# A 128-byte pad among the constants, and one weight load issued ahead of one adaLN load

## The chip, the cores and the metric

The kernel runs on one core of one Trainium2 chip. The metric is the time of one execution on the device in microseconds (us). A second number, the span, is what the profiler saw from the first instruction to the last; what lies around it is the start and end of the program.

## What is computed

A decoder trunk of two layers on 256 tokens of width 2048, all in float32. Cut to what matters here:

```
for layer in range(2):
    shift, scale, gate = split(silu(c) @ ada_w[layer] + ada_b[layer], 3)
    h = x * (1 + scale) + shift
    if layer == 0:
        y = ssd_mixer(h, ...)       # h @ in_w (2048 x 10304), conv, scan, gate, @ out_w
    else:
        y = dilated_mixer(h, ...)   # h @ in_w, attention, gate, @ out_w
    x = layer_norm(ALPHA * x + (1 + gate) * y)
    if layer == 0:
        k, v = split(x @ kv_w, 2)
```

`c` is one vector, so `silu(c) @ ada_w` is a product of a vector with 2 x 3 x 16 tiles of 128 output columns. Everything else of weight is a product of 256 rows with a large matrix.

## The kernel before

**Products.** A product is made from three float32r products: each weight is split into a rounded high half and a remainder, each activation as well, and high x high, high x low and low x high are summed in PSUM. A weight comes as pieces of 128 x 1024 (512 KB), each covering two k-tiles of 128 rows and 512 columns, or four k-tiles and 256 columns. `load_piece` (L86 to L90) puts a piece into one of six buffers `raw`; `split` (L97 to L102) has ScalarE copy it into one of four buffers `whi` (L99) and VectorE subtract that into one of four `wlo` (L101). SyncE's queue issues these loads. `cm_piece` (L150 to L152) and `cm_wide` (L181, L184) hold the weights as the stationary operand and stream the activations `actT`; `tm_mults` (L212 to L214) holds the activations and streams the weights. `SHORT` moves `whi` and `wlo` by 16 elements within their buffers where weights are stationary; `LONG` does not.

**adaLN.** `ada_load` (L287) brings one tile of 128 output columns, 128 x 2048 (1 MB), into `araw`; `ada_dot` (L294) multiplies it on VectorE with `cb_`, silu(c) spread over the partitions, and sums it along the row. `fetch()` issues the next of 32 such loads: scale and shift for k-tile 0, scale and shift for k-tile 1, and so on. `h_step()` takes the next of them in the same order: its dot, and after a shift the two ScalarE steps L499 (h = x * scale + shift) and L501 (its high half into `actT`), then the low half on VectorE (L503).

**The beginning (to about 160 us).** While h is still being made k-tile by k-tile, products are already begun on what is there. A table `order` lists 58 pieces: b4, b6, h, z2, z1, b2, x1, h and so on, where b, x and z are column blocks of in_w and h the two blocks that run along with every k-tile. The first three pieces are loaded in halves (L534, L537). A piece's product that ends before the last k-tile is put away from PSUM by ScalarE (L634, reported there for all of these evictions, first time) or added on VectorE (L632). DMAs are issued in the order of the code, each waiting for the landing of the one eight places before it and for its buffer to be free: loads of `raw` have six buffers, loads of `araw` two buffers in each of two pools. The code just before the loop over `order` writes out the first loads and steps by hand.

**Later stages.** From about 162 us the rest of the first layer (scan, gate, out_w), the shared keys and values, and the second layer follow. Their pieces are loaded and split ahead in the same buffers; gate loads of layer 0 and all adaLN loads of layer 1 run in the background.

**Memory.** Pools lie one behind the other in a partition: first `cons` (`cb_`, `adab`, `prm`, `cc`, `magic`, `mod0`, `mod1`), then `wp` with `raw`, `whi`, `wlo`, then `act` with `actT`, and the rest. In the built kernel the first `raw` begins at byte 28800 of the partition, `whi` at 53376, `wlo` at 70784, `actT` at 88192: each 128 past a multiple of 256. The buffers of `whi` and of `wlo` follow each other at 4352 bytes, 17 x 256. `u0` and `u1` are taken from the other end of the memory.

Of the kernel before, what the change touches and what calls it, by code (L numbers as in the profile page):

```python
# [9 lines left out]
F32 = mybir.dt.float32  # L10
# [8 lines left out]
P = 128  # L19
# [30 lines left out]
def trunk(ctx, tc, xT, x, c, par, cst, bias, lnrow, ada, wdt, win, wxs, wout, wk, wv, wbin, wbout, out):  # L50
# [3 lines left out]
    cons = ctx.enter_context(tc.tile_pool(name="cons", bufs=1))  # L54
# [23 lines left out]
    ident = cc[:, CI:CI + 128]  # L78
    tri = cc[:, CT:CT + 128]
    ones = cc[:, CM:CM + 128]  # L80
    SHORT, LONG = (16, 16), (0, 0)

    def rows(t, b):
# [3 lines left out]
    def load_piece(src):  # L87
        raw = wp.tile([P, 1024], F32, name="raw", bufs=6)
        nc.sync.dma_start(raw, src)
        return raw  # L90
# [194 lines left out]
    def ada_load(pool, layer, kind, ct):  # L285
        raw = pool.tile([P, D], F32, name="araw", bufs=2)
        nc.sync.dma_start(raw, ada[layer, KIND.index(kind), ct])  # L287
        return raw
# [44 lines left out]
    with ExitStack() as cA:  # L333
# [15 lines left out]
        with ExitStack() as cS:  # L349
# [78 lines left out]
            with ExitStack() as c0:  # L428
# [31 lines left out]
                def fetch():  # L460
                    i = len(raws)
                    if i < len(cols):
                        raws.append(ada_load((wp1, pe)[i // 2 % 2], *cols[i]))

                def fetch_x(kt):
                    xts[kt // 2] = pe.tile([P, 2, L], F32, name="xt")
                    (nc.sync if kt else nc.scalar).dma_start(xts[kt // 2], xT[:, kt:kt + 2, :])
# [59 lines left out]
                def fetch_piece():  # L527
                    if len(pieces) < len(order):
                        k, q, _ = order[len(pieces)]
                        pieces.append(load_piece(source[k][q]))  # L530
# [46 lines left out]
                fetch()  # L577
                h_step()
                fetch_piece()
                fetch()  # L580
                fetch_x(2)
                fetch_piece()
                plain.t = h_step.t
                last = plain(1, plain(0, last))
                h_low = late.pop()
# [791 lines left out]
```

## Time and profile before

| | us |
|---|---|
| median of 3 runs | 1236.28 |
| lowest and highest | 1235.71, 1237.11 |
| the profiled execution | 1236.29 |
| its span | 1234.5 |
| TensorE matmul busy in it | 1220.3 |
| VectorE busy | 1028.0 |
| ScalarE busy | 701.6 |

The profile is of one execution. Its engines are PE (matmuls of TensorE), PEld (its weight loads), DVE (VectorE), ACT (ScalarE), POOL (GpSimd) and SP (SyncE, which issues DMAs). In the rows of a timeline the first two numbers are the start and the duration in us, L101 is line 101 of the kernel, x2 two instructions merged, and square brackets tell how long the engine had been idle and what ended that. In a table of windows each row has the stretch, its length, the busy time of each engine with the number of instructions, the granted TensorE clock (PEclk), the busy share of the 16 DMA engines, and what they moved in GB/s.

### The profile page before, as it was taken

The page shows a single profiled execution, that of the slowest core. Times are in us where ns is not written, and L with a number is a line of the kernel's source. Part 1 is how long each engine was busy: PE and PEld are TensorE (multiplying, and loading weights), DVE is VectorE, ACT ScalarE, POOL GpSimd, SP SyncE. Part 2 cuts the span into 40 slices and gives each one's busy share as a digit, 9 for nine tenths or more (in the row PEclk, how much of TensorE's full clock was granted, in tenths as well). Part 3 has the DMA queues.
Part 4 walks back from the last instruction along what each step waited for, and adds up shares of the span by engine and source line. Part 5 has one row for each costly group of instructions (what it writes and reads, how often), then busy time and mean ns, then how long its engine had stood idle before and what let it go on. Part 6 is the DMA issues. An engine that isn't in the chain of part 4 may idle for free.

```text
span 1234.5 us, 18854 instructions
## 1 busy us (share of the span) xinstructions
PE 1220.3 (99%) x7132; PEld 1049.4 (85%) x7132; DVE 1028.0 (83%) x1464; ACT 701.6 (57%) x1048; POOL 3.9 (0%) x8
## 2 busy tenths in 40 slices
PE   8999999999999999999999999999999999999998
PEld 7889988898888888888888788888888888888886
DVE  6899996999988989899778678888978876758776
ACT  3554577878597789754335545344445644445551
POOL 0000000000000000000000000000000000000001
PEclk9999999999999999999999999999999999999999
DMA  9999986687666456599998569989998774464673
GB/s 373 414 414 415 413 283 244 216 305 247 222 204 205 171 172 205 203 337 353 365 316 294 195 204 362 356 341 371 378 382 313 224 261 147 122 201 124 207 256 69
DMA packets 81372, 335.92 MB, mean 272 GB/s; under 512 B 9201, under 2 KB 9985, under 8 KB 68481
## 3 DMA queue, kind: packets, MB, share of 16 engines
q1 hardware_dynamic: 80352, 333.33, 75.0%
q0 software_dynamic: 576, 1.05, 0.6%
q8 instruction: 56, 0.92, 0.3%
q10 hardware_dynamic: 352, 0.34, 0.1%
q14 instruction: 36, 0.29, 0.1%
HBM read 331.45 MB, written 3.23 MB: 271 GB/s over the span
## 4 chain that ended last, share of the span: by engine, by line
PE 84%; DMA 6%; DVE 6%; ACT 2%; issue 1%; ACTq 0%; DVEq 0%
PE acc L181 24%; PE acc L184 12%; PE acc L213 12%; PE acc L214 12%; PE acc L212 12%; DMA raw<-in_win 5%; DVE araw L294 3%; DVE wlo L101 2%; PE py L775 1%; PE acc L150 1%; PE acc L152 1%; PE acc L151 1%; DMA araw<-in_ada 1%; ACT whi L99 1%; PE acc L985 1%
## 5 line engine op out<-in xcount | busy, mean ns | idle before, releaser
L99 ACT ACTIVATE whi<-raw 128x1024 fp32r<-128x1024 f32 x389 | 408.9, 1058 | 362.5 <-PE acc L214 130.7
L101 DVE TENSOR_TENSOR wlo<-raw,whi 128x1024 fp32r<-128x1024 f32 x389 | 469.2, 1221 | 146.8 <-ACT whi L99 139.9
L181 PE MATMUL acc<-actT,whi 128*128 128x512 f32 x1280 | 402.8, 394 | 0.0
L184 PEld LDWEIGHTS acc<-actT,wlo 128*128 128x128 f32 x1280 | 239.5, 188 | 53.5 <-DVE wlo L101 0.5
L213 PE MATMUL acc<-wlo,actT 128*128 128x512 f32 x656 | 257.3, 392 | 1.9 <-DVE wlo L101 1.9
L212 PE MATMUL acc<-whi,actT 128*128 128x512 f32 x656 | 254.0, 394 | 0.0
L184 PE MATMUL acc<-actT,wlo 128*128 128x256 f32 x1280 | 253.8, 280 | 0.0
L294 DVE SCALAR_TENSOR_TENSOR araw<-araw,cb__72 128x2048 f32<-128x2048 f32 x95 | 217.0, 2284 | 5.2 <-DMA araw<-in_ada 4.7
L181 PEld LDWEIGHTS acc<-actT,whi 128*128 128x128 f32 x1280 | 193.9, 188 | 0.4
L214 PE MATMUL acc<-whi,actT 128*128 128x512 f32 x432 | 168.8, 391 | 0.0
L213 PEld LDWEIGHTS acc<-wlo,actT 128*128 128x128 f32 x656 | 123.2, 188 | 28.7 <-DVE wlo L101 3.6
L212 PEld LDWEIGHTS acc<-whi,actT 128*128 128x128 f32 x656 | 122.6, 188 | 25.1 <-ACT s L634 0.8
L150 PE MATMUL acc<-actT,whi 128*128 128x256 f32 x372 | 103.7, 283 | 2.9 <-ACT s L634 2.0
L152 PE MATMUL acc<-actT,wlo 128*128 128x256 f32 x372 | 102.4, 283 | 1.7 <-DVE wlo L101 1.6
L151 PE MATMUL acc<-actT,whi 128*128 128x256 f32 x372 | 103.6, 281 | 0.0
L214 PEld LDWEIGHTS acc<-whi,actT 128*128 128x128 f32 x432 | 81.1, 188 | 16.6
L214 PE MATMUL acc<-whi,ylo 128*128 128x512 f32 x224 | 87.6, 391 | 0.0
L150 PEld LDWEIGHTS acc<-actT,whi 128*128 128x128 f32 x372 | 70.3, 190 | 4.2 <-ACT s L634 2.4
L152 PEld LDWEIGHTS acc<-actT,wlo 128*128 128x128 f32 x372 | 69.5, 190 | 2.7 <-DVE wlo L101 2.7
L151 PEld LDWEIGHTS acc<-actT,whi 128*128 128x128 f32 x372 | 71.3, 192 | 0.2
L214 PEld LDWEIGHTS acc<-whi,ylo 128*128 128x128 f32 x224 | 42.1, 188 | 8.7
L733 ACT ACTIVATE seg<-cbc,cumT 128x128 f32<-128x128 f32 x128 | 41.1, 390 | 2.6 <-PE py L775 2.1
(311 smaller groups left out, 1151.1 us busy)
## 6 DMA issues: line engine op xcount, KB each, us to landing
araw<-in_ada SPq DMA_DIRECT2D x96, 1024.0 KB, 7.4
raw<-in_win SPq DMA_DIRECT2D x109, 512.0 KB, 5.7
raw<-in_wout SPq DMA_DIRECT2D x64, 512.0 KB, 5.8
raw<-in_wbin SPq DMA_DIRECT2D x64, 512.0 KB, 4.0
raw<-in_wxs SPq DMA_DIRECT2D x48, 512.0 KB, 4.4
raw<-in_wv SPq DMA_DIRECT2D x48, 512.0 KB, 6.8
raw<-in_wk SPq DMA_DIRECT2D x48, 512.0 KB, 7.2
cbc<-cumd SPq DMA_DIRECT2D x16, 512.0 KB, 4.9
```

The costliest lines, as they stand in the source:

```text
L99: copied.append(S.activation(hi, raw, AF.Copy))
L101: latest.append(V.tensor_tensor(lo, raw, hi.bitcast(F32), op=ALU.subtract))
L150: T.matmul(o, hi[:, k, c_], ahi[:, kt, :], start=first, stop=False, skip_group_check=True)
L151: T.matmul(o, hi[:, k, c_], alo[:, kt, :], start=False, stop=False, skip_group_check=True)
L152: T.matmul(o, lo[:, k, c_], ahi[:, kt, :], start=False, stop=kt == k1 - 1, skip_group_check=True)
L181: T.matmul(ps[n], hi[:, k, n * P:n * P + P], both(kt), start=kt == 0, stop=False, skip_group_check=True)
L184: T.matmul(ps[n][:, 0, :], lo[:, k, n * P:n * P + P], high(kt), start=False, stop=kt == KT - 1, skip_group_check=True)
L212: T.matmul(o, h_, hi[:, k, :], start=kt == k0, stop=False, skip_group_check=part)
L213: T.matmul(o, h_, lo[:, k, :], start=False, stop=False, skip_group_check=part)
L214: end = T.matmul(o, l_, hi[:, k, :], start=False, stop=kt == k1 - 1, skip_group_check=part)
L294: return V.scalar_tensor_tensor(raw, raw, 1.0, cb_, op0=ALU.mult, op1=ALU.mult, accum_out=mod[layer][:, ct, j:j + 1])
L733: S.activation(seg[:, hh, b, :], cbc[:, hh, b, :], AF.Relu, bias=cumT[:, b, h0 + hh:h0 + hh + 1], scale=-1.0)
```

## The change

Two edits.

```
     ones = cc[:, CM:CM + 128]
+    cons.tile([P, 32], F32, name="pad")
     SHORT, LONG = (16, 16), (0, 0)
...
                 fetch()
                 h_step()
                 fetch_piece()
+                fetch_piece()
                 fetch()
                 fetch_x(2)
-                fetch_piece()
                 plain.t = h_step.t
```

The first adds a tile of 128 bytes per partition, which nothing reads or writes, behind `cc`. Everything allocated behind it moves up by 128 bytes: `raw` begins at 28928, `whi` at 53504, `wlo` at 70912, `actT` at 88320, all multiples of 256. `cb_`, `adab`, `prm`, `cc`, `u0` and `u1` stay where they were. Tiles that stood at other distances move too: with `SHORT`, the stationary weights begin 64 bytes past a multiple of 256 and no longer 192.

The second moves the load of the sixth piece of `order` (b2, k-tiles 0 and 1) ahead of one `fetch()` and of `fetch_x(2)`. By the count of the calls, that `fetch()` is the sixth adaLN load, the shift tile of the third k-tile; the scale tile of the same k-tile has been issued by the `fetch()` between the two `h_step()` calls, and stays ahead.

SyncE's queue, from the fourth piece on. `raw_198` is the fourth piece, `raw_211` the fifth, `raw_217` the sixth, `raw_255` the seventh; `araw_203` is the fifth adaLN load, `araw_213` the sixth, `araw_257` the seventh; `xt_215` is x for k-tiles 2 and 3. Before:

```order
L89 DMA raw_198<-in_win 128x1024
L287 DMA araw_203<-in_ada 128x2048
L89 DMA raw_211<-in_win 128x1024
L287 DMA araw_213<-in_ada 128x2048
L467 DMA xt_215<-in_xT 128x512
L89 DMA raw_217<-in_win 128x1024
L89 DMA raw_255<-in_win 128x1024
L287 DMA araw_257<-in_ada 128x2048
```

After, where the added line makes every line number one larger and the buffers are numbered anew (`raw_214` is the sixth piece, `araw_216` the sixth adaLN load):

```order
L90 DMA raw_199<-in_win 128x1024
L288 DMA araw_204<-in_ada 128x2048
L90 DMA raw_212<-in_win 128x1024
L90 DMA raw_214<-in_win 128x1024
L288 DMA araw_216<-in_ada 128x2048
L468 DMA xt_218<-in_xT 128x512
L90 DMA raw_256<-in_win 128x1024
L288 DMA araw_258<-in_ada 128x2048
```

One load has passed two others; from the seventh piece on the queue is as before.

ScalarE at the same place. `whi_345` is the high half of the sixth piece, `s2` and `sz` are what z2 and z1 are put away into (`acc_322`, `acc_323` and `acc_351`, `acc_352` in PSUM), `htmp_340` is h of k-tile 2. Before:

```order
L99 ACTIVATE whi_318<-raw_211 128x1024
L99 ACTIVATE whi_345<-raw_217 128x1024
L499 ACTIVATE htmp_340<-xt_215,mod0_79 128x256
L634 ACTIVATE s2_95<-acc_322 128x512
L501 ACTIVATE actT_83<-htmp_340 128x256
L634 ACTIVATE s2_95<-acc_323 128x512
L99 ACTIVATE whi_367<-raw_255 128x1024
L634 ACTIVATE sz_113<-acc_351 128x512
L634 ACTIVATE sz_113<-acc_352 128x512
L99 ACTIVATE whi_405<-raw_259 128x1024
```

After:

```order
L100 ACTIVATE whi_319<-raw_212 128x1024
L100 ACTIVATE whi_346<-raw_214 128x1024
L635 ACTIVATE s2_96<-acc_323 128x512
L635 ACTIVATE s2_96<-acc_324 128x512
L100 ACTIVATE whi_368<-raw_256 128x1024
L500 ACTIVATE htmp_341<-xt_218,mod0_80 128x256
L635 ACTIVATE sz_114<-acc_352 128x512
L502 ACTIVATE actT_84<-htmp_341 128x256
L635 ACTIVATE sz_114<-acc_353 128x512
L100 ACTIVATE whi_406<-raw_260 128x1024
```

Putting z2 away now stands right behind the sixth piece's high half, and h of k-tile 2 behind the seventh's.

VectorE there. `wlo_346` is the low half of the sixth piece, `araw_213` the sixth adaLN dot, `mod0` takes its sum. Before:

```order
L101 TENSOR_TENSOR wlo_319<-raw_211,whi_318 128x1024
L294 SCALAR_TENSOR_TENSOR araw_213,mod0_79<-araw_213,cb__72 128x2048
L299 TENSOR_TENSOR mod0_79<-mod0_79,adab_73 128x2
L101 TENSOR_TENSOR wlo_346<-raw_217,whi_345 128x1024
L503 TENSOR_TENSOR actT_83<-htmp_340,actT_83 128x256
L101 TENSOR_TENSOR wlo_368<-raw_255,whi_367 128x1024
L294 SCALAR_TENSOR_TENSOR araw_257,mod0_79<-araw_257,cb__72 128x2048
```

After:

```order
L102 TENSOR_TENSOR wlo_320<-raw_212,whi_319 128x1024
L102 TENSOR_TENSOR wlo_347<-raw_214,whi_346 128x1024
L295 SCALAR_TENSOR_TENSOR araw_216,mod0_80<-araw_216,cb__72 128x2048
L300 TENSOR_TENSOR mod0_80<-mod0_80,adab_73 128x2
L102 TENSOR_TENSOR wlo_369<-raw_256,whi_368 128x1024
L504 TENSOR_TENSOR actT_84<-htmp_341,actT_84 128x256
L295 SCALAR_TENSOR_TENSOR araw_258,mod0_80<-araw_258,cb__72 128x2048
```

The sixth piece's low half has passed the sixth dot and its bias, and the dot of the seventh adaLN load keeps its place behind the seventh piece. On TensorE the products stand in the order of before; only the first two of the sixth piece's accumulators alternate a little differently (24 matmuls of 256 columns either way).

More of the change, by code (lines that the diff above doesn't have):

```diff
@@ L80, in trunk @@
     ones = cc[:, CM:CM + 128]
+    cons.tile([P, 32], F32, name="pad")
     SHORT, LONG = (16, 16), (0, 0)
@@ L579, in trunk @@
                 fetch_piece()
+                fetch_piece()
                 fetch()
                 fetch_x(2)
-                fetch_piece()
                 plain.t = h_step.t
```

## The prediction

> **What bounds the kernel.** The page first: span, engines, the DMA slices, the chain of what ended last.
>
> ```profile
> span 1234.5 us, 18854 instructions
> PE 1220.3 (99%) x7132; PEld 1049.4 (85%) x7132; DVE 1028.0 (83%) x1464; ACT 701.6 (57%) x1048; POOL 3.9 (0%) x8
> ...
> DMA  9999986687666456599998569989998774464673
> ...
> PE 84%; DMA 6%; DVE 6%; ACT 2%; issue 1%; ACTq 0%; DVEq 0%
> ```
>
> The chain is 84% matmuls, so over most of the program TensorE's pace is the time. The DMA row is full in the first five slices (31 us each), so the beginning has another limit. Windows over the beginning and the stage behind it:
>
> ```profile
> 40.00:127.00 87.00, 85.30 (x538) 76.07 (x538) 81.09 (x87) 46.10 (x60) 0.00 (x0) 1.00 1.02 414
> 127.00:162.00 35.00, 33.88 (x273) 32.63 (x272) 33.09 (x37) 17.32 (x22) 0.00 (x0) 1.00 0.99 395
> 162.00:560.00 398.00, 396.88 (x2644) 339.84 (x2643) 360.33 (x615) 308.02 (x520) 0.00 (x0) 1.00 0.68 231
> ```
>
> From 40 to 127 us the DMA engines are never idle (share 1.02, 414 GB/s) and DVE is 93% busy; from 162 on DMA has room and PE does not. The end of the beginning, in the chain by time and in DVE's timeline:
>
> ```profile
> 113.77 13.26 DMA araw<-in_ada
> 127.03 0.02 issue
> 127.05 2.31 DVE araw L294 x2
> ...
> 160.36 1.24 DVE wlo L101
> ```
>
> ```profile
> 46.38 1.22 DVE L101 TENSOR_TENSOR wlo<-raw,whi 128x1024 fp32r<-128x1024 f32 x1
> 47.73 2.29 DVE L294 SCALAR_TENSOR_TENSOR araw<-araw,cb__72 128x2048 f32<-128x2048 f32 x1
> ...
> 124.44 2.50 DVE L101 TENSOR_TENSOR wlo<-raw,whi 128x1024 fp32r<-128x1024 f32 x2
> 127.05 2.29 DVE L294 SCALAR_TENSOR_TENSOR araw<-araw,cb__72 128x2048 f32<-128x2048 f32 x1
> ```
>
> An adaLN load lands at 127.03 and its dot starts at 127.05, 0.11 us after DVE was free (124.44 + 2.50 = 126.94). Behind that, DVE works nearly without a gap to 161.60, and TensorE's unbroken chain starts on that last remainder. The same meeting stands at 47.73, 0.13 us after DVE was free (46.38 + 1.22 = 47.60). So what ends the beginning is the 126 us that a full DMA system needs for everything queued up to that adaLN load, plus 34.6 us of DVE (127.05 to 161.60). The rest, 1073 us, is PE.
>
> **The moved load.** No instruction is added or removed; one issue on SP passes two others. What waits on it, in the timelines of SP and ACT, and of PE (last row):
>
> ```profile
> 16.87 0.33 SPq L287 DMA_DIRECT2D araw<-in_ada  x1
> 17.48 0.33 SPq L467 DMA_DIRECT2D xt<-in_xT  x1
> 18.15 2.19 SPq L89 DMA_DIRECT2D raw<-in_win  x2
> ```
>
> ```profile
> 24.76 1.06 ACT L99 ACTIVATE whi<-raw 128x1024 fp32r<-128x1024 f32 x1 [0.65 <-DMA raw<-in_win]
> 30.17 1.06 ACT L99 ACTIVATE whi<-raw 128x1024 fp32r<-128x1024 f32 x1 [4.35 <-DMA raw<-in_win]
> 31.14 0.58 ACT L499 ACTIVATE htmp<-xt,mod 128x256 f32<-128x256 f32 x1
> 31.63 0.57 ACT L634 ACTIVATE s<-acc 128x512 f32<-128x512 f32 x1
> ```
>
> ```profile
> 32.25 0.38 PE L150 MATMUL acc<-actT,whi 128*128 128x256 f32 x1 [1.95 <-ACT s L634]
> ```
>
> ACT sits 4.35 us before the sixth piece's high half, with z2's eviction (L634, 31.63) queued behind it; PE idles 1.95 us for that eviction. The piece lands behind the sixth adaLN load (1.05 MB) and xt (0.26 MB). At 414 GB/s these are 2.5 and 0.6 us, so it lands about 3.2 us earlier, near 27.0, and its high half ends at 28.1; z2 is put away by 29.3. PE had no work left at 30.30 (32.25 - 1.95), and now has it: 1.95 us back. It gets more, since the stall is followed by a slow clock:
>
> ```profile
> 32.00:34.00 2.00, 1.75 (x9) 1.75 (x10) 0.94 (x3) 2.00 (x5) 0.00 (x0) 0.68 1.04 426
> 34.00:36.00 2.00, 2.00 (x12) 2.00 (x11) 2.00 (x2) 1.78 (x3) 0.00 (x0) 0.50 0.99 404
> 36.00:38.00 2.00, 2.00 (x18) 2.00 (x18) 2.00 (x3) 0.19 (x1) 0.00 (x0) 0.96 1.04 413
> ```
>
> Lost clock: 2 x (0.32 + 0.50 + 0.04) = 1.7 us. PE is then up to 3.7 us earlier at 38 us. The other side: the sixth adaLN load lands 0.52 MB later, 1.3 us, and its dot moves from 28.16 to about 29.4.
>
> ```profile
> 28.16 2.29 DVE L294 SCALAR_TENSOR_TENSOR araw<-araw,cb__72 128x2048 f32<-128x2048 f32 x1 [1.08 <-DMA araw<-in_ada]
> ...
> 33.97 1.23 DVE L101 TENSOR_TENSOR wlo<-raw,whi 128x1024 fp32r<-128x1024 f32 x1 [1.00 <-ACT whi L99]
> 35.11 2.28 DVE L294 SCALAR_TENSOR_TENSOR araw<-araw,cb__72 128x2048 f32<-128x2048 f32 x1
> ```
>
> On DVE the remainder of the sixth piece (1.23) runs before that dot, in a gap. Then dot (to 31.7), bias, and the seventh piece's remainder: its high half follows its landing at 31.4 and ends near 32.5, so the remainder runs to 33.7 and the next dot starts near 34.4 instead of 35.11: 0.7 us ahead. PE's earliness may also spare DVE a wait near 50 us. None of it reaches the end: at 47.73 DVE has only 0.13 us before it meets the landing, at 127.05 only 0.11, and the DMA system moves the same bytes in the same order from the seventh piece on, at a share that was 1.02 already. A lead of 0.7 or of 2 us is waited away at the second meeting. Term: 0 to -0.11 us. The cover is the full DMA queue; were it gone, the lead itself, some 1 to 2 us, would be the gain.
>
> **The pad.** It adds no instruction. It moves every large tile by 128 bytes, and their distances from each other not at all. No tile here stood at a multiple of 256, so the trace has no price; I bound each user by what address it could feel.
>
> DVE and ACT: the dots read `araw` against `cb_`, which stays, so here a distance changes. `araw` stood at two such distances already (128 past a multiple of 256, and 192 in the second pool of the beginning):
>
> ```profile
> L294 DVE SCALAR_TENSOR_TENSOR araw<-araw,cb__72 x95: 2272/2284/2294, 10.7 to 939.9; 128x2048 f32<-128x2048 f32 x95
> ```
>
> All 95 lie within 22 ns. I take nothing; 95 x 0.022 = 2 us either way is the bound, most of it beside PE.
>
> PE: of the cycle of four matmuls that `cm_wide` repeats, and of `tm_mults` in out_w:
>
> ```profile
> 302.00 0.62 PE L181 MATMUL acc<-actT,whi 128*128 128x512 f32 x2
> ...
> 303.39 0.62 PE L181 MATMUL acc<-actT,whi 128*128 128x512 f32 x2
> ...
> 306.16 0.62 PE L181 MATMUL acc<-actT,whi 128*128 128x512 f32 x2
> ```
>
> ```profile
> 599.95 0.39 PE L212 MATMUL acc<-whi,actT 128*128 128x512 f32 x1
> ...
> 600.63 0.39 PE L212 MATMUL acc<-whi,actT 128*128 128x512 f32 x1
> ```
>
> One cycle of the wide product is (306.16 - 302.00) / 6 = 693 ns, one of out_w 680 ns, and both stream 1536 columns. So 13 ns of pace can hang on something, and where the operands begin is a candidate. But the wide product keeps 693 over six cycles, which at four cycles a piece cross into another buffer, 17 x 256 bytes on: the buffer's address from 256 up has no say. The pad changes a bit just below that, for both operands alike. I take nothing, and keep both ends: all 640 wide cycles at 680, or all tm cycles at 693.
>
> DMA: a row of 4 KB now starts at a multiple of 256. The Trainium skill, "DMA: Bandwidth & Descriptors", section "How a descriptor splits into AXI transactions", says a transfer must start at a multiple of 256 and that bytes before a misaligned start still cost beats: an estimate from that page is 132 beats for such a row instead of 128, 3%. If that holds for writes, the page would have the 126 us shrink by 3.8; no row here shows an aligned large load. Against it stands the Trainium skill, "SBUF — State Buffer", whose note on cachelines has 16-byte lines, so that every start here is as good as another. From the rows alone: faster DMA gains only what DVE waits for it, since DVE is busy 81.09 of 87 us. I take nothing.
>
> **Sum.** 0 - 0.1 (moved load) + 0 (pad) on the profiled 1236.29 us, which is the median of the runs (1236.28): **1236.2 us**. Its own range, 1235.2 to 1237.2, is about how far runs of one kernel lie apart.
>
> **Rivals.**
> - *The wide products lose their uneven pace.* For: 693 against 680 for equal columns. Against: the pace ignores the buffer. 640 cycles (1280 of L181, two each) x 13 ns = 8.5 us, all on PE's chain: 1227.7.
> - *DMA rows get quicker.* The landing at 127.03 comes earlier until DVE itself is the limit. DVE's waits for the early loads are 1.08 and 1.00 in the rows above and two meetings of 0.1: about 2.3 us, so 1233.9. Against: DVE at 93% has little to give. It straddles the bound of 0.2%.
> - *Slower: the tm products take the uneven pace.* Place: L212 to L214 behind 162 us, 580 cycles of three by the groups of that stretch (the whole program has 656). Price: 13 ns each, 7.5 us, so 1243.8. It decides from a third of them on (190 x 13 ns = 2.5 us). For: one pace per kind of product shows that the layout can matter. Against: as above.
>
> ```profile
> L213 PE MATMUL acc<-wlo,actT 128*128 128x512 f32 x580 | 227.4, 392 | 0.8 <-DVE wlo L101 0.8
> ```
>
> - *The change isn't what its words say.* Its load passes the third k-tile's second adaLN load, not the first. Passing the first too would hand the piece another 2.5 us and take as much from a dot, behind the same full queue: 1236.2 again.
>
> **Chances.** Forecast 0.59; words and deed differ, same time, 0.04; wide pace 0.11; DMA rows 0.10, half of it past 0.2%; tm pace 0.16. A difference of 0.2%, 2.5 us, is about what a measurement tells from none. So faster 0.11 + 0.05 = 0.16, same 0.59 + 0.04 + 0.05 = 0.68, slower 0.16. The range takes in the DMA case, half of the tm case (to about 1240.5), and leaves out the wide case and the other half: 0.19. It runs from 1231.5, which is the DMA case with another 2 us for the bound on the dots, to 1240.5.
>
> **What would show it.** Right: L99 of the sixth piece near 27 us; no PE wait of 1.95 and no clock of 0.5 near 34; DVE's adaLN dots again starting on a landing at 127; the last remainder before PE's chain near 160.4; 693 and 680 ns per cycle as before. Wrong: a DMA rate over 420 GB/s from 40 to 127 us, or another pace at 302 or 600 us.

## The result and the profile after

The changed kernel takes **1234.53 us** (median of 21 runs, 1233.1 to 1237.16) against 1236.32 for the kernel before (21 runs beside it). The ratio is 0.9986, 95% interval 0.998 to 0.9992: 1.8 us faster, a real difference, and smaller than the 0.2% that the prediction set as its bound. The forecast was 1236.2, the rival with quicker DMA rows 1233.9; the time lies nearer to the rival, and the profile shows that it is the rival that happened.

The page of the profiled execution (1234.27 us) first, span, engines and the DMA slices:

```profile
span 1232.5 us, 18855 instructions
PE 1218.7 (99%) x7132; PEld 1048.2 (85%) x7132; DVE 1027.9 (83%) x1464; ACT 701.7 (57%) x1048; POOL 3.9 (0%) x8
...
DMA  9999977687666456699988569989998774464663
```

The sixth DMA digit has gone from 8 to 7 and the seventh from 6 to 7. A digit is a slice of 31 us, too coarse for what is sought here. The windows of the beginning, with the same columns as before:

```profile
32.00:34.00 2.00, 2.00 (x20) 2.00 (x18) 1.95 (x3) 1.67 (x4) 0.00 (x0) 1.00 1.01 424
34.00:36.00 2.00, 2.00 (x19) 2.00 (x18) 2.00 (x3) 1.06 (x1) 0.00 (x0) 1.00 1.00 416
...
40.00:127.00 87.00, 83.97 (x524) 74.70 (x524) 81.08 (x85) 46.55 (x61) 0.00 (x0) 1.00 1.02 422
127.00:162.00 35.00, 34.32 (x278) 33.23 (x278) 32.63 (x39) 17.88 (x23) 0.00 (x0) 1.00 0.95 379
```

From 40 to 127 us the DMA engines are as full as before (1.02) but move 422 GB/s in place of 414. From 127 us on they have room (0.95), where they had none (0.99). The clock of 0.68 and 0.50 between 32 and 36 us is gone. VectorE's timeline at the two meetings of the prediction, and the last remainder of the beginning:

```profile
46.58 2.29 DVE L295 SCALAR_TENSOR_TENSOR araw<-araw,cb__72 128x2048 f32<-128x2048 f32 x1 [0.45 <-DMA araw<-in_ada]
...
122.92 2.36 DVE L102 TENSOR_TENSOR wlo<-raw,whi 128x1024 fp32r<-128x1024 f32 x2
125.19 2.29 DVE L295 SCALAR_TENSOR_TENSOR araw<-araw,cb__72 128x2048 f32<-128x2048 f32 x1
...
158.51 1.22 DVE L102 TENSOR_TENSOR wlo<-raw,whi 128x1024 fp32r<-128x1024 f32 x1
```

The first meeting still is one: VectorE waits 0.45 us for the landing, which comes 1.15 us earlier than before (46.58 against 47.73). The second is none any more: at 125.19 the dot follows the remainder ahead of it at once. So behind the first meeting no dot of VectorE starts on a landing, up to the last remainder. What VectorE still waits for is mostly ScalarE's high halves: 5.9 us in 11 waits from 46 to 159 us, and 5.9 us in 11 in the kernel before. The last remainder starts at 158.51 in place of 160.36: **1.85 us, the whole of the 1.8 us** between the medians. The dots of the two traces, one against the other, show where it was won: 1.15 us by the first meeting, 0.34 near 107 us, at a meeting that the prediction doesn't have, and the last 0.37 at 127.

```profile
107.46 2.29 DVE L294 SCALAR_TENSOR_TENSOR araw<-araw,cb__72 128x2048 f32<-128x2048 f32 x1
```

```profile
105.97 2.28 DVE L295 SCALAR_TENSOR_TENSOR araw<-araw,cb__72 128x2048 f32<-128x2048 f32 x1
```

Behind the last remainder TensorE's rows are those of before: a wide cycle takes (306.24 - 302.08) / 6 = 693 ns, a cycle of out_w (600.81 - 598.77) / 3 = 680 ns.

```profile
302.08 0.62 PE L182 MATMUL acc<-actT,whi 128*128 128x512 f32 x2
...
306.24 0.62 PE L182 MATMUL acc<-actT,whi 128*128 128x512 f32 x2
```

```profile
598.77 0.39 PE L213 MATMUL acc<-whi,actT 128*128 128x512 f32 x1
...
600.81 0.39 PE L213 MATMUL acc<-whi,actT 128*128 128x512 f32 x1
```

The moved load did its part where it stands. ScalarE's timeline and TensorE's waits from 26 to 52 us:

```profile
26.20 1.06 ACT L100 ACTIVATE whi<-raw 128x1024 fp32r<-128x1024 f32 x1 [0.23 <-DMA raw<-in_win]
27.16 1.26 ACT L635 ACTIVATE s<-acc 128x512 f32<-128x512 f32 x2
```

```profile
37.04 0.39 PE L153 MATMUL acc<-actT,wlo 128*128 128x256 f32 x1 [0.41 <-DVE wlo L102]
40.71 0.39 PE L153 MATMUL acc<-actT,wlo 128*128 128x256 f32 x1 [0.65 <-DVE wlo L102]
```

The sixth piece's high half starts at 26.20 in place of 30.17, and z2 is put away behind it. TensorE's wait of 1.95 us is gone; in its place stand two of 0.41 and 0.65 for VectorE.

Two edits were made at once, so the comparison alone doesn't say whether the order of the transfers or their addresses made the rows quicker.

### The profile page after: what moved, and what is told of

Its sections match the earlier page's. It is cut to its first block, busy times and chain, and to the rows that moved or that the text cites. A ratio compares the mean times of both kernels' runs of the same rounds, so it can differ in the third digit from the quotient of the medians.

```text
span 1232.5 us, 18855 instructions
## 1 busy us (share of the span) xinstructions
PE 1218.7 (99%) x7132; PEld 1048.2 (85%) x7132; DVE 1027.9 (83%) x1464; ACT 701.7 (57%) x1048; POOL 3.9 (0%) x8
## 4 chain that ended last, share of the span: by engine, by line
PE 82%; DVE 7%; DMA 7%; ACT 2%; issue 2%; SPq 0%; DVEq 0%; ACTq 0%
PE acc L182 24%; PE acc L185 12%; PE acc L214 11%; PE acc L215 11%; PE acc L213 11%; DVE araw L295 3%; DMA raw<-in_win 3%; DMA araw<-in_ada 3%; DVE wlo L102 2%; PE acc L153 2%; PE acc L151 2%; PE acc L152 1%; PE py L776 1%; DMA raw<-in_wv 1%; ACT whi L100 1%
```

## Experiments

Each time below is the median of 5 to 11 runs, taken beside the kernel before on the same chip (whose medians were 1236.96, 1236.81 and 1236.48 us for the three groups of runs); ratios are to that kernel. Edits are to the changed kernel unless said otherwise.

### Each edit alone

`pad_alone` is the kernel before with the pad; `move_alone` the changed kernel without it:

```
-    cons.tile([P, 32], F32, name="pad")
```

> The pad without the moved load. Theory rows (the pad makes DMA rows quicker; the moved load adds little): DMA at 421 to 423 GB/s from 40 to 127 us, the last remainder before TensorE's chain at 158.5 to 159.2, and 1234.5 to 1235.1 us. Theory order (the moved load is the gain, and the higher rate comes from the order of the transfers): 414 GB/s, the last remainder at 160.4, 1236.3 us. In both, PE idles about 2 us near 30 us and the clock falls to 0.5 near 34.

> The moved load without the pad. Theory rows: 414 GB/s from 40 to 127 us, an adaLN dot that starts on a landing at 127.0 again, the last remainder at 160.3, 1236.2 us. Theory order: 422 GB/s, the last remainder at 158.5, 1234.5 us. In both the stall near 30 us and the slow clock near 34 are gone.

Measured: the pad alone 1234.81 us, ratio 0.9986 (0.9977 to 0.9995); the moved load alone 1236.56 us, ratio 0.9997 (0.9988 to 1.0006). The window from 40 us and the last remainder, of `pad_alone` first, then of `move_alone` (there with the dot that starts near 127 us):

```profile
40.00:127.00 87.00, 84.65 (x529) 75.15 (x528) 81.52 (x85) 46.93 (x61) 0.00 (x0) 1.00 1.02 422
```

```profile
158.44 1.22 DVE L102 TENSOR_TENSOR wlo<-raw,whi 128x1024 fp32r<-128x1024 f32 x1
```

```profile
40.00:127.00 87.00, 84.41 (x524) 74.65 (x523) 80.93 (x88) 46.42 (x61) 0.00 (x0) 1.00 1.02 414
```

```profile
126.80 2.29 DVE L294 SCALAR_TENSOR_TENSOR araw<-araw,cb__72 128x2048 f32<-128x2048 f32 x1
...
160.13 1.22 DVE L101 TENSOR_TENSOR wlo<-raw,whi 128x1024 fp32r<-128x1024 f32 x1
```

The pad brings the rate and the 1.9 us, with the load where it was; the moved load brings 0.23 us at the last remainder, within what runs differ by. Theory order has fallen, and theory rows holds. What the expectation of `pad_alone` got wrong is the stall: TensorE waited 0.85 us there, not 2, and the clock at 32 to 36 us stayed at 1.00.

```profile
31.18 0.38 PE L151 MATMUL acc<-actT,whi 128*128 128x256 f32 x1 [0.85 <-ACT s L635]
```

### Which tile's start counts

`raw_alone` aligns `raw` and is meant to put the rest back; `rest_alone` leaves `raw`, `whi` and `wlo` and moves what is behind them:

```
 raw_alone                                       rest_alone
+    act.tile([P, 32], F32, name="apad")         -    cons.tile([P, 32], F32, name="pad")
-    SHORT, LONG = (16, 16), (0, 0)              +    act.tile([P, 32], F32, name="apad")
+    SHORT, LONG = (48, 48), (32, 32)
-    def split(..., off=(0, 0)):
+    def split(..., off=(32, 32)):
```

> Moved load; only the six buffers raw begin at multiples of 256, while whi, wlo, actT and all else lie as before the change (whi and wlo are moved back within their buffers, a second pad of 128 bytes stands ahead of actT). Theory each-its-own (a transfer is quick if its own target is): raw has 15.7 of the 36.7 MB from 40 to 127 us, so about 43% of the 8 GB/s, 417 to 418 GB/s, and some 1235.4 us. Theory raw-only (araw at 128 and at 192 past a multiple of 256 costs nothing): 421 to 422 GB/s and 1234.5 us. Theory not-raw: 414 GB/s and 1236.2 us.

> Moved load; the 128 bytes stand behind wlo, ahead of actT, so raw, whi and wlo lie as before the change, and actT, araw, xt and all behind them as after it. Theory each-its-own: the other 57%, 418 to 419 GB/s and some 1235.3 us. Theory raw-only: 414 GB/s and 1236.2 us. Theory not-raw: 422 GB/s and 1234.5 us.

Measured: 1242.2 us, ratio 1.0043 (1.003 to 1.0055), and 1243.1 us, ratio 1.0051 (1.0038 to 1.0063). Both are **slower**, which no theory had. The beginning isn't the cause: the windows from 40 us of `raw_alone` and of `rest_alone` show the full rate in the first and some of the gain in the second.

```profile
40.00:127.00 87.00, 84.43 (x528) 74.93 (x527) 81.44 (x85) 46.59 (x61) 0.00 (x0) 1.00 1.02 422
```

```profile
40.00:127.00 87.00, 83.98 (x514) 74.01 (x515) 80.38 (x85) 45.35 (x59) 0.00 (x0) 1.00 1.02 417
```

Theory each-its-own has fallen here: the one kernel has all 8 GB/s of the gain, the other 3 of them. Theory raw-only has the 422 but not the 417. What 417 means comes under "Other pads".

The loss is in the products that stream weights. TensorE's timeline of `raw_alone` in out_w:

```profile
598.98 0.39 PE L213 MATMUL acc<-whi,actT 128*128 128x512 f32 x1
...
601.07 0.39 PE L213 MATMUL acc<-whi,actT 128*128 128x512 f32 x1
```

Three cycles take 2.09 us, 697 ns each, in place of 680. That is the case of the prediction's slower rival, met by accident. In `raw_alone` one helper that hands out the weights' buffers (`first_or`) kept its default offset, so in `tm_chunk` the streamed weights began at 0 and the activations at 128 past a multiple of 256; in `rest_alone` it was 128 and 0. In all kernels with 680 ns the two begin alike modulo 256. `raw_only` is `raw_alone` with the default mended; `all_but_raw` is `raw_only` without the pad among the constants, so that all but `raw` begin as in the changed kernel modulo 256:

```
-    def first_or(src, q, off=(0, 0)):
+    def first_or(src, q, off=(32, 32)):
```

> As raw_alone, with the offset mended: there the streamed weights of the later stages began at 0 and the activations at 128 past a multiple of 256, here both begin at 128 past one again, as in the kernel before. Theory distance (TensorE's pace in the products that stream weights hangs on the distance of the two operands modulo 256 bytes: 227 ns for 512 columns at 0, 232 at 128): 227 again everywhere, and with 422 GB/s and the last remainder at 158.2 the time is 1234.5 us. Theory absolute (the pace hangs on where the operands themselves begin, which moved by 256 bytes): 232 again and 1242 us.

> The moved load; all tiles as in the changed kernel modulo 256, except that raw begins at 128 past a multiple of 256 as before the change. Theory distance: 227 ns everywhere. Theory raw (where raw begins sets the rate of all transfers of the beginning): 417 GB/s as in rest_alone, the last remainder at 159.0, 1235.1 us. Theory whi (whi and wlo set it, which moved along in raw_alone): 422 GB/s and 1234.5 us.

Measured: `raw_only` 1234.8 us, ratio 0.9987 (0.9978 to 0.9995); `all_but_raw` 1235.54 us, ratio 0.9993 (0.9984 to 1.0001). TensorE's timeline of `raw_only` in out_w, and the windows of `raw_only` and of `all_but_raw`:

```profile
598.80 0.39 PE L213 MATMUL acc<-whi,actT 128*128 128x512 f32 x1
...
600.85 0.39 PE L213 MATMUL acc<-whi,actT 128*128 128x512 f32 x1
```

```profile
40.00:127.00 87.00, 84.46 (x527) 74.96 (x527) 81.40 (x88) 46.72 (x62) 0.00 (x0) 1.00 1.02 422
```

```profile
40.00:127.00 87.00, 84.26 (x526) 74.72 (x526) 81.36 (x85) 46.18 (x61) 0.00 (x0) 1.00 1.02 418
```

Theory distance holds: 683 ns a cycle again and 7.4 us less than `raw_alone`, by one default offset; over the 580 cycles behind the beginning that is 12.8 ns each on average (17 in the stretch shown), the rival's price of 13. With only `raw` at a multiple of 256 the rate is the full 422 and the median that of the changed kernel; with all but `raw` there it is 418. That is what theory raw expected, but it isn't yet the rule, as the next section shows.

The last remainder missed its expectation in both traces: 159.81 in `raw_only`, not 158.2, and 160.25 in `all_but_raw`, not 159.0.

```profile
159.81 1.22 DVE L102 TENSOR_TENSOR wlo<-raw,whi 128x1024 fp32r<-128x1024 f32 x1
```

```profile
160.25 1.23 DVE L101 TENSOR_TENSOR wlo<-raw,whi 128x1024 fp32r<-128x1024 f32 x1
```

The profiled executions took 1235.77 and 1236.35 us, 1.0 and 0.8 more than the medians. `raw_only` is 1.62 us behind the changed kernel by the dot near 30 us (30.53 against 28.91), and stays 1.3 behind; `all_but_raw` loses 1.3 us between 141 and 148. One execution's remainder so differs by over 1 us at one and the same rate, and the verdicts here rest on the rates and the medians.

### Other pads

The pad's size in the changed kernel, all distances kept:

```
-    cons.tile([P, 32], F32, name="pad")
+    cons.tile([P, 8], F32, name="pad")      # pad_32; 16: pad_64; 48: pad_192
```

> The changed kernel with a pad of 32 bytes: all tiles behind the constants begin 160 past a multiple of 256 (and xt and half of the early araw 224), no distance between them changes. Theory 256 (only multiples of 256 for raw are free): 414 GB/s as with 128, last remainder at 160.2, 1236.3 us. Theory 64 (what counts is multiples of 64, and 128 is a special case): another rate than 414, slower if rows that begin inside a unit of 64 pay more: 405 to 412 GB/s and 1237 to 1239 us.

> A pad of 64 bytes: raw and the rest begin 192 past a multiple of 256, the pool of xt and half of the early araw at 0. Theory 256: 414 to 418 GB/s (the araw at 0 may help as in all_but_raw), 1235.5 to 1236.3 us. Theory graded (the cost follows from how many bytes lie ahead of the next multiple of 256: 64 here, 128 before): between 414 and 422 GB/s in the middle. Theory 128 (only a start at 128 or 160 past a multiple of 256 pays): 422 GB/s and 1234.5 us.

> A pad of 192 bytes: raw and the rest begin 64 past a multiple of 256. Theory 256: 414 GB/s and 1236.3 us. Theory graded: 192 bytes lie ahead of the next multiple, so below 414. Theory 128: 422 GB/s and 1234.5 us, since xt and half of the early araw stand at 64 in the changed kernel at no cost.

Measured, with the starts in bytes past a multiple of 256 (for the early `araw`, its two pools), rates from the window of 40 to 127 us:

| kernel | raw | araw | GB/s | us | ratio |
|---|---|---|---|---|---|
| move_alone | 128 | 128, 192 | 414 | 1236.56 | 0.9997 |
| pad_32 | 160 | 160, 224 | 414 | 1236.2 | 0.9999 |
| pad_192 | 64 | 64, 128 | 414 | 1236.09 | 1.0 |
| pad_64 | 192 | 192, 0 | 418 | 1235.12 | 0.9988 |
| all_but_raw | 128 | 0, 64 | 418 | 1235.54 | 0.9993 |
| raw_only | 0 | 128, 192 | 422 | 1234.8 | 0.9987 |
| changed kernel | 0 | 0, 64 | 422 | 1234.53 | 0.9986 |

Windows of `pad_192` and of `pad_64`:

```profile
40.00:127.00 87.00, 83.89 (x522) 74.17 (x523) 80.55 (x85) 46.06 (x60) 0.00 (x0) 1.00 1.02 414
```

```profile
40.00:127.00 87.00, 83.96 (x520) 73.67 (x519) 80.39 (x85) 45.73 (x60) 0.00 (x0) 1.00 1.02 418
```

Theory 256 takes all seven. Theory 64 had 405 to 412 for `pad_32`, theory 128 would have had 422 in `pad_64` and `pad_192`, and theory graded would have put `pad_192` below 414. A start of `raw` at 64, 128 or 160 costs the same; with half of the early `araw` at 0 half of the cost goes; with `raw` at 0 all of it, wherever `araw` stands.

That half goes shows what theory raw leaves out. In the trace's packet records of `all_but_raw` from 40 to 127 us, about 82% of the rows of those `araw` loads whose tiles begin at 0 take the 309 ns of the changed kernel, and about 10% of those whose tiles begin at 64; in `raw_only` it is 98% in either pool, though neither begins at 0. So a row of `araw` is slow where its own start and that of `raw` are both off, and one of the two at 0 is enough. A later stretch with full DMA engines has all four cases, since the `araw` tiles used there begin alike: windows of the kernel before (`raw` and `araw` at 128), of `all_but_raw` (128 and 0), of `raw_only` (0 and 128) and of the changed kernel (0 and 0).

```profile
580.00:590.00 10.00, 10.00 (x46) 8.28 (x45) 8.43 (x9) 4.25 (x4) 0.00 (x0) 1.00 1.02 415
580.00:590.00 10.00, 9.89 (x44) 7.85 (x43) 8.51 (x9) 4.25 (x4) 0.00 (x0) 1.00 1.02 422
580.00:590.00 10.00, 10.00 (x45) 8.25 (x46) 8.51 (x8) 4.26 (x4) 0.00 (x0) 1.00 1.02 423
580.00:590.00 10.00, 10.00 (x46) 8.26 (x45) 8.51 (x8) 4.81 (x5) 0.00 (x0) 1.00 1.03 424
```

Only the first, with both off, is slow: 56% of its packets of 8192 bytes take 309 ns or less, and 99% or more in the other three. In the same stretch the other kernels with both off (`move_alone`, `pad_32`, `pad_64`, `pad_192`) have 413 to 415 GB/s, `raw_alone` and `rest_alone` 418 and 419. No run has all of the early `araw` at 0 beside a `raw` that is off; to judge by this stretch, it would have brought the full rate as well.

### What bounds the beginning now

`fewer_xt` takes work from the DMA system. It leaves out loads that the result needs, so its h is not the right one; only its time is of use:

```
+                    if kt > 2:
+                        xts[kt // 2] = xts[1]
+                        return
                     xts[kt // 2] = pe.tile([P, 2, L], F32, name="xt")
```

> The changed kernel without six of the eight loads of x for h (1.6 MB, 3.7 us at 422 GB/s); the h of k-tiles 4 to 15 is made from the x of k-tiles 2 and 3. Theory VectorE (with the quicker rows VectorE alone bounds the beginning from 47 us on): only the wait of 0.45 us ahead of the dot at 46.58 goes, last remainder at 158.0 to 158.5, 1234.0 to 1234.5 us. Theory DMA (transfers still bound it): the last remainder at 155 to 156.5, 1231 to 1232.5 us.

Measured 1233.61 us, ratio 0.9976 (0.9967 to 0.9985). Its last remainder:

```profile
157.97 1.23 DVE L102 TENSOR_TENSOR wlo<-raw,whi 128x1024 fp32r<-128x1024 f32 x1
```

3.7 us of transfers less, and the remainder comes 0.54 us earlier than in the changed kernel. Theory DMA has fallen. VectorE, with its waits for ScalarE, bounds the beginning now; a still quicker DMA would bring half a microsecond at that point, or about 1 us by the medians (1234.53 - 1233.61).

### The other distance

The distance that costs `tm_mults` 13 ns suggested the distance of the wide products as well, 64 - 0 in the changed kernel. `rest_alone` had 192 and 0 there.

```
 short_48: SHORT, LONG = (48, 48), (0, 0)
 wide_48:  SHORT, LONG, WIDE = (16, 16), (0, 0), (48, 48)   # WIDE in cm_wide and in the loads ahead for it
```

> The changed kernel with SHORT = (48, 48) in place of (16, 16): the stationary weights begin 192 past a multiple of 256, the activations stay at 0. In rest_alone they had that distance (192 and 0), and a cycle of the wide product took 689 ns. Theory distance: 689 in place of 693 ns, 640 cycles, 2.2 to 2.6 us less than the changed kernel, 1232.0 to 1232.3 us. Theory absolute: no change, 1234.5 us.

> The changed kernel with offset (48, 48) for the weights of the wide products alone; cm_piece keeps (16, 16). In short_48 the wide cycle was 689 ns, but the quad products of 230 to 430 us and the beginning streamed 256 columns in 117.8 ns where they had 114 to 117 before. Theory distance: the wide gain of 2.2 us without that loss, 1232.2 to 1232.6 us, 1 us under short_48. Theory no more (what short_48 gained is all there is): 1233.4 us.

Measured: `short_48` 1233.43 us, ratio 0.9976 (0.9966 to 0.9986); `wide_48` **1232.55 us, ratio 0.9968 (0.9956 to 0.9981)**, which is less than either kernel. `short_48` missed both of its theories, 1232.0 to 1232.3 and 1234.5. TensorE's timeline of `wide_48`:

```profile
302.20 0.62 PE L182 MATMUL acc<-actT,whi 128*128 128x512 f32 x2
...
304.96 0.62 PE L182 MATMUL acc<-actT,whi 128*128 128x512 f32 x2
```

Four cycles take 2.76 us, 690 ns each in place of 693. In the trace they alternate between 687 and 692 ns, and the mean of all 640 is 689.9 against 693.2 in the changed kernel. 640 x 3.3 ns is 2.1 us; 2.0 us against the changed kernel's median came out. `short_48` moves `cm_piece` along with the wide products and gained 1.1 by the medians. `wide_48` leaves it alone and stands 0.9 us lower, as theory distance had it, though the two intervals overlap.

## Why the prediction was right, and where it was wrong

- **What bounds the kernel** was right in the main: a beginning that ends where a full DMA system and a 93% busy VectorE meet, then TensorE. It has a third meeting, near 107 us. The 1.85 us that the beginning lost is what the kernel lost.
- **The moved load** was right in its verdict. Alone it is worth 0.23 us at the last remainder and nothing that the median can tell, since the dots still start on landings (126.80 in `move_alone`). Sizes were off: the sixth piece came 4.0 us earlier, not 3.2; its high half started at 26.20, not near 27; the dot behind it moved by 0.75 us (28.91), not 1.3. TensorE's lead went into two waits of 1.06 us together.
- **The slow clock** as a follow-up of the stall is not shown: of all the traces taken it is in that of before alone, and `pad_alone` had a stall of 0.85 us there with the clock at 1.00 behind it.
- **The pad, TensorE and VectorE**: right. No pace of TensorE changed, for the reason given, that both operands moved alike; `raw_alone` and `rest_alone` show that the pace does hang on their distance. The argument that buffers 17 x 256 bytes apart keep one pace fits too: such a step leaves the distance modulo 256 alone.
- **The pad, DMA: here the forecast failed.** It put "I take nothing" on the start of a DMA row, held that faster rows gain only what VectorE waits for, and gave that 0.10. The rows did get quicker, and the bound was then near in size: 2.3 us of waits expected, 1.85 gone. In part that is luck: 2.1 of the 2.3 are waits ahead of 36 us and 0.1 stands for each meeting, where 0.34 and 0.37 went at 107 and 127 alone. The verdict (no difference past 0.2%) held although its mechanism didn't: it rests on what VectorE had to wait, and for quicker rows the prediction itself gave that an even chance of going past 0.2%. In the packet counts (packets, MB, share of 16 engines) of the DMA queue from 40 to 127 us, before and after:

```profile
q1 hardware_dynamic: 7818, 35.93, 101.8%
```

```profile
q1 hardware_dynamic: 7925, 36.59, 101.6%
```

16 x 87 us x 1.018 / 35.93 MB = 39.4 ns of an engine for a kilobyte before, 16 x 87 x 1.016 / 36.59 = 38.6 after: 2.0% less.

- The Trainium skill, "DMA: Bandwidth & Descriptors", section "How a descriptor splits into AXI transactions", had this right in kind, that a start off a multiple of 256 can cost. The prediction's estimate from it was 3% for a row of 4 KB, and 2% was measured over all rows. Its rule takes each transfer by itself and charges the bytes ahead of the start. The runs agree with neither: in `raw_only` `araw` stands at 128 and 192, and the rate is the full 422; a start of `raw` at 64 cost what one at 128 did, 414 GB/s in both. The Trainium skill's note on 16-byte lines in "SBUF — State Buffer", section "Door 1: The DMA port swizzle", weighed against it, says nothing of this: starts at 64, 128 and 160 are multiples of 16, and all were slow where `araw` was off as well.
- **Two sums** are slightly off. 640 cycles x 13 ns are 8.3 us, not 8.5, and the DMA case less 2 us is 1231.9, not 1231.5. Neither changes a verdict.

What should have tipped it: 414 GB/s at a share of 1.02 was a full system whose rate stood in no relation to another start, because the trace had no aligned large load. An untried address next to a resource that is full deserved more than one chance in ten.

## What to carry to other kernels

Where DMA is full, look up where its largest targets begin within a partition; here a pad of 128 bytes was worth 2% of the rate, and it would have been enough to put one of the two streams that run together at multiples of 256. What such a gain is worth at the end is the sum of the waits for landings on the engine behind it, since that engine is the next bound. Alignment and distance are two things: move tiles that one matmul reads together, or measure the pace of its products again.

## What the runs showed of the hardware

- Rows of two streams of loads slow each other where both begin off a multiple of 256 bytes: 414 GB/s with `raw` and `araw` off, 417 and 418 with half of the early `araw` at 0, 422 with `raw` at 0. From 40 to 127 us, packets of 8192 bytes, which are rows of `araw`, take 316.2 ns on average before, 309.3 in the changed kernel and 309.7 in `raw_only`, whose `araw` is no better aligned than before. With `raw` off and `araw` at 0 the stretch of 580 to 590 us has 422 GB/s, so a start of one stream alone off a multiple costs nothing that these windows tell. How one row's start reaches another's packet isn't settled.
- TensorE's pace hangs on the distance of its two operands modulo 256 bytes. Products that stream 512 columns of weights over held activations: 680 ns for three at distance 0, 697 at 128. The wide products: 693 ns a cycle with the weights 64 past the activations, 690 at 192 past them. Other distances weren't tried for either.
